# Decoder layer with 32 experts: tail order, last turn and gate product moved

## The chip, the core and the metric

The kernel runs on one core of a Trainium2 chip. The metric is device time in microseconds of one execution of the whole layer. TensorE (PE) multiplies, VectorE (DVE) and ScalarE (ACT) work on tiles elementwise, GpSimd (POOL) does elementwise work and issues the indirect DMAs, SyncE (SP) issues the loads of weights.

## What is computed

One decoder layer on 512 tokens of 1024 features, float32 (cut to the steps that matter here):

```python
proj = x @ w_in                                   # 1024 x 2048
mix = concat(pool_mixer(..), conv_mixer(..)) @ w_out
x = layer_norm(ALPHA * x + mix, ln1_g, ln1_b)
# top 4 of 32 experts per token, softmax over the chosen logits
gu = xb @ w_gate_up[e] + b_gate_up[e]             # 1024 x 2048
gate = min(gu[:, :1024], 7.0)
up = clip(gu[:, 1024:], -7.0, 7.0)
y = ((up + 1) * (gate * sigmoid(1.702 * gate))) @ w_down[e] + b_down[e]
x = layer_norm(ALPHA * x + sum of gate-weighted y, ln2_g, ln2_b)
g = sigmoid(x @ ple_gate_w + ple_gate_b)
x = layer_norm(ALPHA * x + g * (p @ ple_proj), ln3_g, ln3_b)
```

## The kernel before

**Precision and chunks.** Every float32 product is made of three float32r products: an operand is cast to a high part, the rest is its low part, and `mm3` (lines 212 to 214) issues high x low, low x high and high x high. Weights arrive in chunks of 1 MB (128 x 2048) through a ring of 14 buffers. `split` turns a chunk into two parts: ScalarE casts it (line 114) and VectorE subtracts (line 117, the "chunk subtraction"); `split(later=True)` gives the subtraction back to be called later. `ahead(j)` gives chunk j's buffers free, loads further chunks and splits as many as the lookahead allows. The order of instructions on each engine is the order of the program (a hand-made schedule), so where a call stands decides what waits behind what.

**Start.** Four token tiles of x are turned on PE (`turned`, line 309) into the high part `xh` and the low part `xl`, through two PSUM buffers of the tag `tr`; `columns` multiplies a block of w_in with them.

**Experts.** For each expert e up to 96 token rows are gathered (`gather`, line 315, GpSimd), turned by PE (`split_t`) and multiplied with 8 gate/up chunks (k = 0 to 7). `act` yields in steps: the gate is limited (`gm`, VectorE, line 337), `up` is copied (`h`, ScalarE, line 340) and clipped (GpSimd, line 341), `sg` is the sigmoid (ScalarE, line 346), the product `gm * sg` (line 347) runs on GpSimd, and VectorE finishes `h` (line 349). While that goes on, `down(e - 1)` multiplies the expert before with its 4 down chunks (j = 0 to 3, two column halves n each), and `emit` weighs the result into `yo` and adds it to `acc` in HBM by an indirect DMA (the "scatter", line 357). `h` of expert e is turned at k = 2 of expert e + 1. The last expert has no next one: it does `up` and the product on VectorE, and `last_turn` turns its `h` between `down(30)` and `down(31)`, with 3 warm matmuls ahead and 9 behind (`keep_warm`, line 208: matmuls whose result nobody reads).

**Side steps.** `tables` makes the index tables of the next experts in three steps; `embed_parts` turns the embedding input p in five steps (first `pgb`, then a tile each) in experts 19 and 20.

**Tail.** `embed(i)` is 12 matmuls, p times ple_proj for token tile i, `embedded` copies it out of PSUM. Then comes a loop with a run-time count (`further_blocks`, for experts with more than 96 rows; it runs zero times here), which every engine and all DMAs must have reached before it is left. Behind it the sums are read from `acc` into `x2`, `combine` adds the down bias, `second` is the second normalisation, `turn2` turns the tile, `gate` and `gated` multiply with ple_gate_w, `third` is the last normalisation.

Of the kernel before, what the change touches and what calls it, by code (L numbers as in the profile page):

```python
# [20 lines left out]
P = 128  # L21
# [4 lines left out]
E = 32  # L26
# [12 lines left out]

WARM_START, WARM_ROUTE, WARM_TURN, WARM_END = (6, 7, 7), (2, 2, 2), (3, 9), 10  # L40
TURN1 = 5
# [7 lines left out]
def tile_layer(ctx: ExitStack, tc: tile.TileContext, x, p, w_in, pool_mix, pool_scale, conv_w, w_out,  # L49
# [282 lines left out]

    def act(gp, up, work, mul=nc.gpsimd):

        gp, up = (q.rearrange("p a b -> p (a b)") for q in (gp, up))
        gm, h = work("gm"), work("h")
        nc.vector.tensor_scalar(gm, gp, LIMIT, None, op0=ALU.min)  # L337
        yield h
        if mul is nc.gpsimd:
            nc.scalar.copy(h, up)  # L340
            mul.tensor_scalar(h, h, LIMIT, -LIMIT, op0=ALU.min, op1=ALU.max)  # L341
        else:
            nc.vector.tensor_scalar(h, up, LIMIT, -LIMIT, op0=ALU.min, op1=ALU.max)
        yield
        sg = work("sg")
        nc.scalar.activation(sg, gm, AF.Sigmoid, scale=SW_ALPHA)  # L346
        mul.tensor_mul(gm, gm, sg)  # L347
        yield
        nc.vector.scalar_tensor_tensor(h, h, 1.0, gm, op0=ALU.add, op1=ALU.mult)  # L349
# [18 lines left out]
    with tc.tile_pool(name="mix", bufs=1, side=RIGHT) as q:  # L368
# [6 lines left out]
        with tc.tile_pool(name="xin", bufs=1, side=RIGHT) as xp:  # L375
# [17 lines left out]

            def columns(o, cs, b, ts_):

                wh, wl = (parts[cs[b]] if len(cs) == 2 else (q[:, :, b * P:(b + 1) * P] for q in parts[cs[0]]))
                for k in range(ND):
                    mm3(o[:, b, ts_], wh[:, k], wl[:, k], xh[:, k, ts_], xl[:, k, ts_], k == 0, k == ND - 1)

# [7 lines left out]
            o1 = big()  # L407
            columns(o1, c_in[0], 0, slice(0, 256))
            turned(2)
            turned(3)  # L410
            columns(o1, c_in[0], 1, slice(0, 256))
            for b in range(2):
# [443 lines left out]

    def embedded(i, o, halves=False):
        if halves:
            nc.scalar.copy(ple[i][:, :512], o[:, 0])
            nc.vector.tensor_copy(ple[i][:, 512:], o[:, 1])  # L860
        else:
            nc.scalar.copy(ple[i], o.rearrange("p a b -> p (a b)"))


    hs, hT = {}, {}

    def down(e, after={}, before={}):
        ah, al = hT.pop(e)
        o = big(CAP)
        for j in range(4):  # L870
            wh, wl = parts.pop(c_dn[e][j])
            for n in range(2):
                ns = slice(n * 512, (n + 1) * 512)
                for b in range(2):
                    k = 2 * j + b
                    mm3(o[:, n], ah[:, k], al[:, k], wh[:, b, ns], wl[:, b, ns], k == 0, k == ND - 1)
            for f in before.get(j, ()):
                f()
            if e == E - 2 and j == 2:
                done(c_dn[e][j])  # L880
            elif e < E - 1 or j < 3:
                ahead(c_dn[e][j])
            for f in after.get(j, ()):
                f()
# [4 lines left out]
    def last_turn():  # L889
        keep_warm(WARM_TURN[0], bsp[:, :P], bsp[:, :512])  # L890
        hT[E - 1] = split_t(hs.pop(E - 1), "x", mp1, 1)
        keep_warm(WARM_TURN[1], bsp[:, :P], bsp[:, :512])

# [11 lines left out]
    for e in range(E):  # L905
# [7 lines left out]
        for k in range(ND):  # L913
            wh, wl = parts.pop(c_gu[e][k])
            for o, n, c in halves:
                cs = slice(c, c + 512)
                mm3(o[:, n], ah[:, k], al[:, k], wh[:, 0, cs], wl[:, 0, cs], False, k == ND - 1)
            if k < ND - 1 or e:
                kept = ahead(c_gu[e][k], int(e == E - 1 and k == 0))
# [13 lines left out]
            if k == (0 if e == E - 1 else 1):  # L933
                steps = (tables(2, mp1) if e == 0 else tables(0, mp1) if e == 1 else
                         tables(e + 2, mp1) if e % 2 == 0 and e + 2 < E else
                         further() if e == 5 else prepare() if e == E - 1 else iter(()))
            if k in ((1, 2, 4) if e < E - 1 else (0, 1, 4, 5, 6)):
                next(steps, None)
            if (e, k) == (EMBED + 1, 0):
                embed_steps = embed_parts()  # L940
            if (e, k) in ((EMBED + 1, 0), (EMBED + 1, 1), (EMBED + 1, 4), (EMBED + 1, 5), (EMBED + 2, 0)):
                next(embed_steps, None)
        last = e == E - 1
        if e and not last:
            xT[e + 1] = split_t(xg.pop(e + 1), "x", mp1, 1)
        steps_h = act(gp, up, lambda n: mp2.tile([P, F], F32, tag=n, name=n)[:CAP], nc.vector if last else nc.gpsimd)
        hs[e] = next(steps_h)
        if not last:
            next(steps_h)
        if e == 0:  # L950
# [12 lines left out]
        if last:  # L963
            limit[0] = len(chunks)
            down(e - 1, {0: [finish, finish, finish]}, {3: [last_turn]})
        elif e:
            down(e - 1, {0: [multiply], 1: [gather_next], 2: [finish]})
        else:
            multiply()
            gather_next()  # L970
# [23 lines left out]
    later = []  # L994
    down(E - 1, {2: [lambda: later.append(split(later=True))]})
    later[0]()
    lookahead[0] = 5
    splits(1)
    embedded(0, embed(0))
    o1, o2 = embed(1), embed(2)  # L1000
    last_part = split(later=True)
    embedded(1, o1)
    embedded(2, o2, True)

# [63 lines left out]

    combine(0)
    combine(1)  # L1070
    o3 = embed(3)
    keep_warm(WARM_END, bsp[:, :P], bsp[:, :512], tr([P, 512]))
    last_part()
    second(0)
    embedded(3, o3)
    parts.pop(c_pp)
    done(c_pp)
    turn2(0)
    second(1)
    for i in range(NT):  # L1080
# [45 lines left out]
```

## Time and profile before

| What | Value |
|---|---|
| Median of 3 runs | 1420.75 us (1419.46 to 1421.67) |
| Profiled execution, its own time | 1419.95 us |
| Its span, first to last instruction | 1418.1 us |
| PE busy | 1390.6 us, 98% |
| VectorE busy | 1235.8 us, 87% |
| ScalarE busy | 949.6 us, 67% |
| GpSimd busy | 446.4 us, 31% |
| DMA | 464.43 MB, mean 327 GB/s |
| Granted PE clock, mean | 0.995 of full |

Busy time is a share of the whole span; a stage can be bound by another engine than the mean tells, so the rows further down are read stage by stage. Start times in them count from the start of the span. Several matmuls overlap in PE's pipeline, so the distance from start to start is what one costs.

### The profile page before, as it was taken

The page shows a single profiled execution, that of the slowest core. Times are in us where ns is not written, and L with a number is a line of the kernel's source. Part 1 is how long each engine was busy: PE and PEld are TensorE (multiplying, and loading weights), DVE is VectorE, ACT ScalarE, POOL GpSimd, SP SyncE. Part 2 cuts the span into 40 slices and gives each one's busy share as a digit, 9 for nine tenths or more (in the row PEclk, how much of TensorE's full clock was granted, in tenths as well). Part 3 has the DMA queues.
Part 4 walks back from the last instruction along what each step waited for, and adds up shares of the span by engine and source line. Part 5 has one row for each costly group of instructions (what it writes and reads, how often), then busy time and mean ns, then how long its engine had stood idle before and what let it go on. Part 6 is the DMA issues. An engine that isn't in the chain of part 4 may idle for free.

```text
span 1418.1 us, 17667 instructions
## 1 busy us (share of the span) xinstructions
PE 1390.6 (98%) x6616; PEld 994.3 (70%) x6616; DVE 1235.8 (87%) x1050; ACT 949.6 (67%) x741; POOL 446.4 (31%) x201
## 2 busy tenths in 40 slices
PE   9999999999999999999999999999999999999896
PEld 8788766666666666666666666666666666666675
DVE  6645589999999999999989998999999999999785
ACT  5321267777777777777777777777777777777631
POOL 1101124355455555555542231222222222221200
PEclk9999999999999999999999999999999999999998
DMA  9327889999999999999889999999999999999421
GB/s 331 122 89 238 327 330 350 362 383 380 367 376 385 366 380 376 375 371 379 308 311 346 385 389 358 373 377 370 377 377 379 364 379 371 375 377 340 122 90 45
DMA packets 98071, 464.43 MB, mean 327 GB/s; under 512 B 9424, under 2 KB 19168, under 8 KB 65216
## 3 DMA queue, kind: packets, MB, share of 16 engines
q1 hardware_dynamic: 86784, 428.12, 78.3%
q0 software_dynamic: 9536, 33.44, 9.5%
q10 hardware_dynamic: 1664, 1.72, 0.5%
q8 instruction: 54, 0.88, 0.2%
q14 instruction: 33, 0.27, 0.0%
HBM read 443.97 MB, written 19.27 MB: 327 GB/s over the span
## 4 chain that ended last, share of the span: by engine, by line
PE 88%; DVE 6%; issue 4%; DMA 1%; ACT 1%; POOL 0%; DVEq 0%; SPq 0%; ACTq 0%; POOLq 0%
PE big L212 27%; PE big L214 26%; PE big L213 26%; PE tr L309 4%; PE big L1050 3%; DVE ring11dt.float32r L117 1%; PE big L911 1%; DMA acc<-yo,idxs 1%; DVE ring0dt.float32r L117 1%; DVE ring1dt.float32r L117 1%; DVE ring13dt.float32r L117 1%; DVE ring3dt.float32r L117 1%; DVE ring12dt.float32r L117 1%; DMA xs<-in_x_dram 0%; PE tr L571 0%
## 5 line engine op out<-in xcount | busy, mean ns | idle before, releaser
L341 POOL TENSOR_SCALAR h<-h 96x1024 f32<-96x1024 f32 x31 | 39.8, 1283 | 572.4 <-ACT h L340 572.4
L357 POOL DMA_INDIRECT acc<-yo,idxs x32 | 178.9, 5589 | 90.9 <-ACT yo L356 84.0
L214 PE MATMUL big<-chunk,xh 128*96 128x512 f32 x480 | 189.1, 394 | 0.0
L213 PE MATMUL big<-chunk,xl 128*96 128x512 f32 x480 | 188.5, 393 | 0.0
L347 POOL TENSOR_TENSOR gm<-gm,sg 96x1024 f32<-96x1024 f32 x31 | 103.7, 3346 | 65.8 <-ACT sg L346 64.0
L214 PE MATMUL big<-chunk,hh 128*96 128x512 f32 x268 | 105.5, 394 | 0.0
L213 PE MATMUL big<-chunk,hl 128*96 128x512 f32 x268 | 105.5, 394 | 0.0
L214 PEld LDWEIGHTS big<-chunk,xh 128*96 128x96 f32 x480 | 77.1, 161 | 33.2
L213 PEld LDWEIGHTS big<-chunk,xl 128*96 128x96 f32 x480 | 77.4, 161 | 31.0
L315 POOL DMA_INDIRECT xg<-x1d,idxg x31 | 91.8, 2960 | 21.9 <-DVE idxg L655 13.7
L214 PEld LDWEIGHTS big<-chunk,hh 128*96 128x96 f32 x268 | 43.4, 162 | 19.2
L213 PEld LDWEIGHTS big<-chunk,hl 128*96 128x96 f32 x268 | 43.3, 162 | 17.6
L346 ACT ACTIVATE sg<-gm 96x1024 f32<-96x1024 f32 x32 | 34.0, 1061 | 17.9 <-DVE gm L337 13.8
L324 ACT CAST xh<-tr 128x384 fp32r<-128x384 f32 x64 | 27.5, 480 | 24.5 <-PE tr L309 24.5
L117 DVE TENSOR_TENSOR ring12dt.float32r<-ring12dt.float,ring6dt.float32r 128x2048 fp32r<-128x2048 f32 x14 | 35.3, 2521 | 7.8 <-ACT ring6dt.float32r L114 7.8
L356 ACT ACTIVATE yo<-big,gs 96x1024 f32<-96x1024 f32 x31 | 34.5, 1111 | 10.9 <-PE big L214 10.9
L349 DVE SCALAR_TENSOR_TENSOR h<-h,gm 96x1024 f32<-96x1024 f32 x32 | 38.7, 1211 | 2.6 <-POOL gm L347 2.6
L324 ACT CAST hh<-tr 128x384 fp32r<-128x384 f32 x62 | 26.6, 479 | 18.4 <-PE tr L309 18.4
L337 DVE TENSOR_SCALAR gm<-big 96x1024 f32<-96x1024 f32 x32 | 38.7, 1210 | 0.0
L117 DVE TENSOR_TENSOR ring9dt.float32r<-ring9dt.float,ring2dt.float32r 128x2048 fp32r<-128x2048 f32 x14 | 34.7, 2481 | 4.3 <-ACT ring2dt.float32r L114 4.3
L117 DVE TENSOR_TENSOR ring3dt.float32r<-ring3dt.float,ring10dt.float32r 128x2048 fp32r<-128x2048 f32 x14 | 34.7, 2481 | 4.0 <-ACT ring10dt.float32r L114 4.0
L117 DVE TENSOR_TENSOR ring1dt.float32r<-ring1dt.float,ring8dt.float32r 128x2048 fp32r<-128x2048 f32 x14 | 34.7, 2481 | 3.7 <-ACT ring8dt.float32r L114 3.7
(585 smaller groups left out, 4430.4 us busy)
## 6 DMA issues: line engine op xcount, KB each, us to landing
ring13dt.float<-in_w_gate_up_dram SPq DMA_DIRECT2D x18, 1024.0 KB, 7.1
ring10dt.float<-in_w_gate_up_dram SPq DMA_DIRECT2D x18, 1024.0 KB, 7.2
ring1dt.float<-in_w_gate_up_dram SPq DMA_DIRECT2D x18, 1024.0 KB, 6.9
ring2dt.float<-in_w_gate_up_dram SPq DMA_DIRECT2D x18, 1024.0 KB, 7.5
ring3dt.float<-in_w_gate_up_dram SPq DMA_DIRECT2D x18, 1024.0 KB, 8.0
ring4dt.float<-in_w_gate_up_dram SPq DMA_DIRECT2D x18, 1024.0 KB, 7.7
ring9dt.float<-in_w_gate_up_dram SPq DMA_DIRECT2D x17, 1024.0 KB, 7.3
ring5dt.float<-in_w_gate_up_dram SPq DMA_DIRECT2D x17, 1024.0 KB, 7.2
```

The source lines that it names most:

```text
L117: second()
L212: nc.tensor.matmul(o, ah, bl, start=start, stop=False)
L213: nc.tensor.matmul(o, al, bh, start=False, stop=False)
L214: nc.tensor.matmul(o, ah, bh, start=False, stop=stop)
L309: nc.tensor.transpose(t[:, k, :], src[:, (4 * h + k) * P:(4 * h + k + 1) * P], ident[:n, :n])
L315: nc.gpsimd.indirect_dma_start(out=xg, out_offset=None, in_=x1d, in_offset=bass.IndirectOffsetOnAxis(ap=idxg[:, e:e + 1], axis=0))
L324: nc.scalar.copy(hi[:, 4 * h:4 * h + 4], t)
L337: nc.vector.tensor_scalar(gm, gp, LIMIT, None, op0=ALU.min)
L341: mul.tensor_scalar(h, h, LIMIT, -LIMIT, op0=ALU.min, op1=ALU.max)
L347: mul.tensor_mul(gm, gm, sg)
L357: nc.gpsimd.indirect_dma_start(out=acc, out_offset=bass.IndirectOffsetOnAxis(ap=idx, axis=0), in_=y, in_offset=None, compute_op=ALU.add)
L1050: nc.tensor.matmul(o, q[a + k // 4][:, k % 4], ws[k // 2][b][:, k % 2, c0:c1], start=False, stop=b == 1 and k == ND - 1)
```

## The change

Five things are edited. `act` has one form for all experts: ScalarE copies `up`, GpSimd clips it, and the product of gate and sigmoid is VectorE's, a step after the sigmoid. `last_turn` is called within the last down chunk of expert 30, between its two column halves, without warm matmuls. In the tail two embedding tiles stand ahead of the run-time loop and two behind; of the three last chunk splits, the subtractions stand behind the last scatter, one ahead of the loop and two behind it. At the start, token tiles 2 and 3 are turned within `columns`. The steps of `embed_parts` and the third table step of expert 0 stand at other k.

```diff
-WARM_START, WARM_ROUTE, WARM_TURN, WARM_END = (6, 7, 7), (2, 2, 2), (3, 9), 10
+WARM_START, WARM_ROUTE, WARM_END = (6, 7, 7), (2, 2, 2), (8, 3)
...
-        if mul is nc.gpsimd:
-            nc.scalar.copy(h, up)
-            mul.tensor_scalar(h, h, LIMIT, -LIMIT, op0=ALU.min, op1=ALU.max)
-        else:
-            nc.vector.tensor_scalar(h, up, LIMIT, -LIMIT, op0=ALU.min, op1=ALU.max)
+        nc.scalar.copy(h, up)
+        nc.gpsimd.tensor_scalar(h, h, LIMIT, -LIMIT, op0=ALU.min, op1=ALU.max)
         yield
         sg = work("sg")
         nc.scalar.activation(sg, gm, AF.Sigmoid, scale=SW_ALPHA)
-        mul.tensor_mul(gm, gm, sg)
+        yield
+        nc.vector.tensor_mul(gm, gm, sg)
...
-            columns(o1, c_in[0], 0, slice(0, 256))
-            turned(2)
-            turned(3)
-            columns(o1, c_in[0], 1, slice(0, 256))
+            columns(o1, c_in[0], 0, slice(0, 256), {4: 2})
+            columns(o1, c_in[0], 1, slice(0, 256), {2: 3})
...
     def last_turn():
-        keep_warm(WARM_TURN[0], bsp[:, :P], bsp[:, :512])
         hT[E - 1] = split_t(hs.pop(E - 1), "x", mp1, 1)
-        keep_warm(WARM_TURN[1], bsp[:, :P], bsp[:, :512])
...
-            if k in ((1, 2, 4) if e < E - 1 else (0, 1, 4, 5, 6)):
+            if k in ((0, 1, 4, 5, 6) if e == E - 1 else (1, 2, 4 if e else 6)):
                 next(steps, None)
...
-            if (e, k) in ((EMBED + 1, 0), (EMBED + 1, 1), (EMBED + 1, 4), (EMBED + 1, 5), (EMBED + 2, 0)):
+            if (e, k) in ((EMBED + 1, 0), (EMBED + 1, 4), (EMBED + 1, 5), (EMBED + 3, 4), (EMBED + 3, 5)):
                 next(embed_steps, None)
...
-            down(e - 1, {0: [finish, finish, finish]}, {3: [last_turn]})
+            down(e - 1, {0: [finish] * 3}, {(3, 0): [last_turn]})
         elif e:
-            down(e - 1, {0: [multiply], 1: [gather_next], 2: [finish]})
+            down(e - 1, {0: [multiply], 1: [multiply, gather_next], 2: [finish]})
...
     down(E - 1, {2: [lambda: later.append(split(later=True))]})
-    later[0]()
-    lookahead[0] = 5
-    splits(1)
-    embedded(0, embed(0))
-    o1, o2 = embed(1), embed(2)
-    last_part = split(later=True)
-    embedded(1, o1)
-    embedded(2, o2, True)
+
+    embedded(0, embed(0), nc.vector.tensor_copy)
+    lookahead[0] = 5
+    later.append(split(later=True))
+    o = embed(1)
+    later.append(split(later=True))
+    embedded(1, o)
+    later[0]()
+    keep_warm(WARM_END[0], bsp[:, :P], bsp[:, :512], tr([P, 512]))
...
     combine(0)
+    o2 = embed(2)
+    embedded(2, o2)
     combine(1)
     o3 = embed(3)
-    keep_warm(WARM_END, bsp[:, :P], bsp[:, :512], tr([P, 512]))
-    last_part()
+    keep_warm(WARM_END[1], bsp[:, :P], bsp[:, :512], tr([P, 512]))
+    later[1]()
     second(0)
     embedded(3, o3)
...
     turn2(0)
+    later[2]()
     second(1)
```

The rows that follow are instructions in program order of one engine: line, operation, output<-inputs, shape.

VectorE in a late expert (27), from the limit of the gate (`gm`) to the finished `h`; the `ring` rows are chunk subtractions. Before:

```order
L337 TENSOR_SCALAR gm<-big 96x1024
L117 TENSOR_TENSOR ring10dt.float32r<-ring10dt.float_83,ring12dt.float32r 128x2048
L117 TENSOR_TENSOR ring1dt.float32r<-ring1dt.float_65,ring8dt.float32r 128x2048
L117 TENSOR_TENSOR ring2dt.float32r<-ring2dt.float_67,ring13dt.float32r 128x2048
L349 SCALAR_TENSOR_TENSOR h<-h,gm 96x1024
```

And after:

```order
L337 TENSOR_SCALAR gm<-big 96x1024
L117 TENSOR_TENSOR ring10dt.float32r<-ring10dt.float_83,ring12dt.float32r 128x2048
L117 TENSOR_TENSOR ring1dt.float32r<-ring1dt.float_65,ring8dt.float32r 128x2048
L345 TENSOR_TENSOR gm<-gm,sg 96x1024
L117 TENSOR_TENSOR ring2dt.float32r<-ring2dt.float_67,ring13dt.float32r 128x2048
L347 SCALAR_TENSOR_TENSOR h<-h,gm 96x1024
```

The product now stands on VectorE between two chunk subtractions, and the second of these behind it.

PE from the last down chunk of expert 30 to the first of expert 31: `hh` and `xh` are the turned h of expert 30 and 31, `tr` the transposes. Before:

```order
L212 MATMUL big<-ring0dt.float32r,hh 96x512
L213 MATMUL big<-ring3dt.float32r,hl 96x512
L214 MATMUL big<-ring3dt.float32r,hh 96x512
L208 MATMUL big<-bsp 128x512 x3
L309 MATMUL tr<-ident,h 128x96 x8
L208 MATMUL big<-bsp 128x512 x9
L212 MATMUL big<-ring6dt.float32r,xh 96x512
```

And after:

```order
L309 MATMUL tr<-ident,h 128x96 x8
L212 MATMUL big<-ring0dt.float32r,hh 96x512
L213 MATMUL big<-ring3dt.float32r,hl 96x512
L214 MATMUL big<-ring3dt.float32r,hh 96x512
L212 MATMUL big<-ring0dt.float32r,hh 96x512
L213 MATMUL big<-ring3dt.float32r,hl 96x512
L214 MATMUL big<-ring3dt.float32r,hh 96x512
L212 MATMUL big<-ring6dt.float32r,xh 96x512
```

The eight transposes moved ahead of six products of expert 30, and the twelve warm matmuls are gone.

VectorE from the last `yo` (which the last scatter sends) to the sums of token tile 1; the rows of the run-time loop are left out. Before:

```order
L354 TENSOR_SCALAR yo_1441<-big,gs 96x512
L996 TENSOR_TENSOR ring10dt.float32r<-ring10dt.float_83,ring9dt.float32r 128x2048
L117 TENSOR_TENSOR ring1dt.float32r<-ring1dt.float_65,ring11dt.float32r 128x2048
L860 COPY after<-big 128x512
...
L1073 TENSOR_TENSOR ring2dt.float32r<-ring2dt.float_67,ring3dt.float32r 128x2048
L276 SCALAR_TENSOR_TENSOR x_9739,mv<-x_9739,big 128x512 x2
...
L1040 TENSOR_TENSOR turned_9799<-tr,turned_9797 128x512
L1040 TENSOR_TENSOR turned_9800<-tr,turned_9798 128x512
L276 SCALAR_TENSOR_TENSOR x_9740,mv<-x_9740,big 128x512 x2
```

And after:

```order
L352 TENSOR_SCALAR yo_1441<-big,gs 96x512
L856 COPY after<-big 128x1024
L999 TENSOR_TENSOR ring10dt.float32r<-ring10dt.float_83,ring9dt.float32r 128x2048
...
L1072 TENSOR_TENSOR ring1dt.float32r<-ring1dt.float_65,ring11dt.float32r 128x2048
L276 SCALAR_TENSOR_TENSOR x_9719,mv<-x_9719,big 128x512 x2
...
L1037 TENSOR_TENSOR turned_9786<-tr,turned_9784 128x512
L1037 TENSOR_TENSOR turned_9787<-tr,turned_9785 128x512
L1078 TENSOR_TENSOR ring2dt.float32r<-ring2dt.float_67,ring3dt.float32r 128x2048
L276 SCALAR_TENSOR_TENSOR x_9720,mv<-x_9720,big 128x512 x2
```

Of the three chunk subtractions one stayed ahead of the loop, behind the copy of embedding tile 0, and two stand behind the loop, the last of them between the turned tile 0 and the sums of tile 1.

## Rows read from the trace of the kernel before

**Rows 1.** Windows: us; busy (count) of PE, PEld, DVE, ACT, POOL; PE clock; DMA.

```profile
380.70:737.12 356.42, 356.42 (x1681) 248.37 (x1680) 335.23 (x226) 268.86 (x190) 185.03 (x40) 1.00 0.99 369
887.13:1245.72 358.59, 357.25 (x1683) 248.17 (x1682) 333.87 (x227) 271.32 (x191) 91.11 (x43) 1.00 1.00 374
860.10:864.00 3.90, 3.90 (x14) 2.71 (x15) 3.06 (x3) 0.48 (x1) 0.00 (x0) 0.62 1.03 432
```

**Rows 2.** PE's waits, longest first: total us, times, longest.

```profile
PE big L1023 <- issue: 4.3, 1, 4.3
PE tr L309 <- DVE p L845: 2.5, 1, 2.5
PE tr L309 <- DVE xl L391: 1.0, 1, 1.0
PE tr L309 <- DVE tabsb L623: 0.7, 1, 0.7
```

**Rows 3.** The chain that ended last: first and last of its 15 late subtractions.

```profile
773.03 3.67 DVE ring11dt.float32r L117
1279.58 3.64 DVE ring11dt.float32r L117
```

**Rows 4.** Timeline of VectorE, GpSimd and TensorE in one late expert.

```profile
1170.51 3.25 POOL L347 TENSOR_TENSOR gm<-gm,sg 96x1024 f32<-96x1024 f32 x1 [2.39 <-ACT sg L346]
1174.04 2.74 POOL L315 DMA_INDIRECT xg<-x1d,idxg  x1 [0.27 <-POOL gm L347]
1172.26 3.66 DVE L117 TENSOR_TENSOR ring1dt.float32r<-ring1dt.float,ring8dt.float32r 128x2048 fp32r<-128x2048 f32 x1 [0.78 <-ACT ring8dt.float32r L114]
1175.85 2.28 DVE L117 TENSOR_TENSOR ring2dt.float32r<-ring2dt.float,ring13dt.float32r 128x2048 fp32r<-128x2048 f32 x1
1178.82 0.40 PE L212 MATMUL big<-ring2dt.float32r,xh 128*96 128x512 f32 x1
```

**Rows 5.** Timeline around the last h and the last down products.

```profile
1317.74 0.85 PE L208 MATMUL big<-bsp 128*128 128x512 f32 x3
1319.03 2.32 PE L208 MATMUL big<-bsp 128*128 128x512 f32 x9
1318.96 0.86 ACT L324 CAST xh<-tr 128x384 fp32r<-128x384 f32 x2 [4.26 <-PE tr L309]
1321.67 2.29 DVE L117 TENSOR_TENSOR ring11dt.float32r<-ring11dt.float,ring9dt.float32r 128x2048 fp32r<-128x2048 f32 x1 [1.07 <-ACT ring9dt.float32r L114]
1324.01 0.47 PE L212 MATMUL big<-ring11dt.float32r,xh 128*96 128x512 f32 x1
```

**Rows 6.** Timeline around the last scatter, and the earlier scatter of expert 29.

```profile
1334.03 2.28 DVE L996 TENSOR_TENSOR ring10dt.float32r<-ring10dt.float,ring9dt.float32r 128x2048 fp32r<-128x2048 f32 x1
1336.22 2.28 DVE L117 TENSOR_TENSOR ring1dt.float32r<-ring1dt.float,ring11dt.float32r 128x2048 fp32r<-128x2048 f32 x1
1285.29 1.48 POOL L357 DMA_INDIRECT acc<-yo,idxs  x1 [4.23 <-ACT yo L356]
1334.38 5.42 POOL L357 DMA_INDIRECT acc<-yo,idxs  x1 [6.91 <-DVE yo L354]
1341.41 0.69 DVE L860 COPY after<-big 128x512 f32<-128x512 f32 x1 [2.91 <-ACT after L859]
```

**Rows 7.** The chain that ended last, at the last scatter.

```profile
1334.38 9.23 DMA acc<-yo,idxs
```

**Rows 8.** Timeline behind the run-time loop.

```profile
1345.06 1.53 PE L1023 MATMUL big<-bd,gt 96*128 96x512 f32 x4 [4.30 <-issue]
1352.71 1.25 PE L309 MATMUL tr<-ident,x 128*128 128x128 f32 x8
1355.22 0.68 DVE L276 SCALAR_TENSOR_TENSOR x<-x,big 128x512 f32<-128x512 f32 x1
1358.95 1.41 DVE L300 SCALAR_TENSOR_TENSOR x<-work,mv,after 128x512 f32<-128x512 f32 x2 [0.67 <-POOL mv L293]
1359.91 1.23 PE L309 MATMUL tr<-ident,x 128*128 128x128 f32 x8
```

More of the change, by code (lines that the diff above doesn't have):

```diff
@@ L331, in split_t, with act @@
         return both
-    def act(gp, up, work, mul=nc.gpsimd):
+    def act(gp, up, work):
         gp, up = (q.rearrange("p a b -> p (a b)") for q in (gp, up))
@@ L392, in turned, with columns @@
                 transposed(xs[i], P, put)
-            def columns(o, cs, b, ts_):
+            def columns(o, cs, b, ts_, between={}):
                 wh, wl = (parts[cs[b]] if len(cs) == 2 else (q[:, :, b * P:(b + 1) * P] for q in parts[cs[0]]))
                 for k in range(ND):
+                    if k in between:
+                        turned(between[k])
                     mm3(o[:, b, ts_], wh[:, k], wl[:, k], xh[:, k, ts_], xl[:, k, ts_], k == 0, k == ND - 1)
@@ L855, in embed, with embedded, down @@
         return o
[L857 to L862, printed above, removed]
+    def embedded(i, o, copy=nc.scalar.copy):
+        copy(ple[i], o.rearrange("p a b -> p (a b)"))
     hs, hT = {}, {}
-    def down(e, after={}, before={}):
+    def down(e, after={}, between={}):
         ah, al = hT.pop(e)
@@ L876, in down @@
                     mm3(o[:, n], ah[:, k], al[:, k], wh[:, b, ns], wl[:, b, ns], k == 0, k == ND - 1)
-            for f in before.get(j, ()):
-                f()
+                for f in between.get((j, n), ()):
+                    f()
             if e == E - 2 and j == 2:
@@ L917, in tile_layer @@
                 mm3(o[:, n], ah[:, k], al[:, k], wh[:, 0, cs], wl[:, 0, cs], False, k == ND - 1)
-            if k < ND - 1 or e:
+            if (e, k) == (E - 1, ND - 1):
+                done(c_gu[e][k])
+            elif k < ND - 1 or e:
                 kept = ahead(c_gu[e][k], int(e == E - 1 and k == 0))
@@ L945, in tile_layer @@
             xT[e + 1] = split_t(xg.pop(e + 1), "x", mp1, 1)
-        steps_h = act(gp, up, lambda n: mp2.tile([P, F], F32, tag=n, name=n)[:CAP], nc.vector if last else nc.gpsimd)
+        steps_h = act(gp, up, lambda n: mp2.tile([P, F], F32, tag=n, name=n)[:CAP])
         hs[e] = next(steps_h)
-        if not last:
-            next(steps_h)
+        next(steps_h)
+        if last:
+            splits()
         if e == 0:
@@ L964, in tile_layer @@
             limit[0] = len(chunks)
-            down(e - 1, {0: [finish, finish, finish]}, {3: [last_turn]})
+            down(e - 1, {0: [finish] * 3}, {(3, 0): [last_turn]})
         elif e:
-            down(e - 1, {0: [multiply], 1: [gather_next], 2: [finish]})
+            down(e - 1, {0: [multiply], 1: [multiply, gather_next], 2: [finish]})
         else:
+            multiply()
             multiply()
```

## The prediction

> **What bounds the kernel now.** I read the windows first: two stretches of ten experts, one early and one late [rows 1]. In the early one PE is busy for all of its 356.42 us at the full clock; in the late one it is busy for 357.25 of 358.59 us. So the experts are bound by TensorE, and a change helps only where PE waits or does filler work. Next I read PE's waits [rows 2]: 4.3 us behind the run-time loop, 2.5 us in the expert that turns the embedding input, 1.0 us at the start, 0.7 us in expert 0. Third, the chain that ended last [rows 3]: it stays on PE except at 15 points, one per expert from 773 to 1280 us, where a chunk subtraction of VectorE takes about 3.65 us instead of the usual 2.28. Last I read the timeline at the end, where the last scatter must land before the sums can be read back, and that is where filler matmuls stand.
>
> **Gate product on VectorE.** The timeline of one late expert shows why that subtraction is long [rows 4]. GpSimd's product runs from 1170.51 to 1173.76; the subtraction has started at 1172.26 and ends at 1175.92, 2.16 after the product's end, which is nearly its whole own length. It was held, not slowed. The change takes the product off GpSimd (3.25) and puts one on VectorE (an estimate of 1.2: half the width of a subtraction of 2.28). VectorE gives 3.66 - 2.28 = 1.38 back and gets 1.2, so its load hardly changes. What matters is the order: the held subtraction now ends at about 1174.54, before PE asks for it, and the product comes behind it. The next one, of ring2, then starts at about 1175.7 instead of 1175.85, and PE needs it at 1178.82. The gain is the difference of the two stretches: (358.59 - 356.42)/10 = 0.22 per expert, 15 times: **-3.3**. Bounds: 0, if another wait steps in, and -3.3, since PE is busy throughout the early stretch and no more is to be had. The gather now waits for VectorE's product, but its rows are wanted only at the end of the next expert.
>
> **Embedding input turned later.** In expert 19 the second piece (a cast, a subtraction, two transposes) no longer follows right behind the first. PE waited 2.5 us there for a transpose buffer [rows 2], and for 3.90 us behind it PE ran at a granted clock of 0.62 [rows 1], which loses 3.9 x 0.38 = 1.5. The pieces now stand at k = 4 and 5 of experts 19 and 21; in the kernel before, two stood at k = 4 and 5 of 19, and no wait of PE is listed for them. **-4.0**, bounds -2.5 and -4.3.
>
> **Start and expert 0.** The transposes of the last two x tiles are spread between column products, with 18 products between the two, so the buffers are free again: the 1.0 wait goes. The table step of expert 0 moves from k = 4 to 6, behind the transposes that waited 0.7 for its buffer. **-1.7**, bounds 0 and -2.7 (two shorter waits near by).
>
> **The last h.** Twelve warm matmuls go. From 1317.74 to 1324.01 lie 12 of them, 8 transposes (some 0.6) and 12 products [rows 5], so each is about 0.23 and the twelve are 2.8. But the second down chunk gives only part of it back: its subtraction starts at 1321.67 and ends at 1323.96, and PE takes it at 1324.01, at once. That subtraction hangs on a cast of ScalarE that stood idle 4.26 us for the transposes. They move up by six products and three warm matmuls, 2.1. Against that h gets a longer way: ScalarE copies it, GpSimd clips it, and two chunk subtractions stand before the product; I reckon h ready about 0.2 behind the point where PE wants it. **-1.9**, bounds 0 and -2.8.
>
> **The last scatter.** It takes GpSimd 5.42, while two chunk subtractions run back to back on VectorE until 1338.50; it ends 1.30 later. An earlier scatter, beside the step that finishes h, took 1.48 [rows 6]. So I read that the subtractions hold it. They now stand behind: one after the copy of embedding tile 0 out of PSUM, which itself waits for 12 matmuls (2.8) behind the last down product, and two after the run-time loop. That would end the scatter 3.9 earlier, and its landing, 9.23 behind its start [rows 7], with it. The Trainium skill's page "SBUF — State Buffer", section "Who interferes with whom", speaks against this: there a tensor-tensor operation takes only the shared read side, while descriptors of GpSimd's DMAs need the write side (the page marks that as inferred), and none was seen to stall. By that page this term is 0. The row stands nearer to this case, so I take most of 3.9.
>
> The loop's exit also wants every engine. The last to arrive before is VectorE's copy, until 1342.10 [rows 6]; after, it is PE. Its filler ended at 1340.76 before (1345.06 less 4.30 idle) [rows 8]; 32 matmuls in place of 36, begun 1.9 earlier, end at about 1337.9. If arrival decides, both steps together give 4.2; if the landing decides, 1.9 + 3.9 = 5.8. I take **-5.0** for last h and scatter together. Behind the loop PE now does 4 + 24 + 3 matmuls instead of 4 + 12 + 10, 31 x 0.23 = 7.1, with a wait of about 0.8 between for a copy out of the buffer that the last tile takes; from 1345.06 to 1352.71 it had 7.65, so this term is near 0, and up to +1.5 if the clock falls there as it did in expert 19.
>
> **The subtraction behind the first turned tile.** Before, VectorE starts the sums of tile 1 at 1355.22, without a gap, and ends them at 1360.36; PE asked for them at 1359.91 [rows 8]. One chunk subtraction (2.28, pitch 2.2) is now in front of them. Nothing covers it: PE waits about 2.1 longer. **+2.1**, bounds 0 and +2.3.
>
> **Sum.** -3.3 - 4.0 - 1.7 - 5.0 + 2.1 = -11.9. The profiled execution took 1419.95 (span 1418.1 and 1.85 around it), so 1408.05; it lies 0.8 under the median of 1420.75, so I forecast 1408.8.
>
> **Rivals.** (a) The subtractions do not hold the scatter, as that page would have it. For it: another cause of 5.42 isn't excluded by one row. Against it: the end 1.30 behind the last subtraction. Then 3.1 of the 5.0 is lost (last h alone remains): 1411.9. (b) The loop's gain is not had, because VectorE, busy 333.87 of 358.59, lets another subtraction come late: 1412.1. (c) The sums of tile 1 come in time, since PE is later there than I think: 1406.7. (d) **Slower**: GpSimd's gather now begins when the product on VectorE ends, beside the ring2 subtraction, and takes the memory side first, as the product did. That subtraction would then be held by up to 2.74, end at about 1180.6 and make PE wait 1.8 in each expert without slack, 15 times: +27, less the 8.6 of the other terms, 1439. It decides from 0.6 us of wait per expert on. Against it: the gather before (1174.04 to 1176.78) runs beside that same subtraction, which takes its plain 2.28 [rows 4]. (e) The change doesn't do what it says, but in expert 19: the late subtractions stay late (0 for -3.3), the start's wait moves on to the next buffer (0 for -1.7), h comes late by all that the warm matmuls gave and the scatter isn't freed (0 for -5.0). Then -4.0 + 2.1 is left, 1418.8, no change.
>
> **Chances.** Forecast with its own spread 0.61, (a) 0.15, (b) 0.09, (c) 0.08, (d) 0.04, (e) 0.03. The range takes in the forecast, (a), (b) and (c): 1404.5 ((c) with the loop's exit by the landing, -0.8, and the lower bounds of start and expert 19, -1.3) to 1413.5 ((a) with a fall of the clock behind the loop, 1.5). About 0.2% (2.8 us) is what a measurement of this kernel can tell from no change: faster 0.93, same 0.03, slower 0.04.
>
> **What would show it.** In the late stretch, chunk subtractions of 2.28 and none of 3.6, and 356.4 us for ten experts. No wait for the embedding input near 857 and no low clock behind it. The last scatter at about 1.5 on GpSimd and the loop left some 5 earlier. Then a wait of about 2 at the second turned tile, as the one step that costs. The forecast is wrong if the last scatter still takes over 4, if a late subtraction stays over 3, or if PE shows new waits per expert.

## The result and the profile after

| What | Before | After |
|---|---|---|
| Median, us | 1420.49 (1419.46 to 1421.67) | 1411.35 (1411.05 to 1414.0) |
| Ratio to before | | 0.994 (0.9928 to 0.9952) |
| Profiled execution, own time | 1419.95 | 1411.42 |
| Its span | 1418.1 | 1409.6 |
| PE busy | 1390.6 | 1388.1 |
| VectorE busy | 1235.8 | 1228.7 |

The change gives 9.1 us. The forecast was 1408.8, 2.6 us lower, in a range from 1404.5 to 1413.5. By the time alone the result lies nearer to the rivals (a), 1411.9, and (b), 1412.1, than to the forecast, so the profile has to tell them apart. PE's waits after the change (wait, total, times, longest):

```profile
PE big L1020 <- issue: 2.3, 1, 2.3
PE tr L309 <- issue: 2.0, 1, 2.0
...
PE big L903 <- ACT h L339: 0.7, 1, 0.7
PE big L212 <- ACT after L856: 0.6, 1, 0.6
...
PE tr L640 <- DVE xl L325: 0.6, 1, 0.6
```

Of the waits of before [rows 2], those for the embedding input, for the low part of x and for the table are gone (one of 0.6 has come at the table's own matmuls, line 640), and the one behind the loop fell from 4.3 to 2.3. A new one of 2.0 stands at the transposes, "issue", since the profile saw no release for it: the second turned tile.

The start of an expert's bias products on PE is a good mark, since it is the same four matmuls in both kernels. Experts 2, 17, 19, 20 and 31, before:

```profile
240.17 0.70 PE L911 MATMUL big<-bsp,sel 64*96 64x512 f32 x4
...
775.91 0.70 PE L911 MATMUL big<-bsp,sel 64*96 64x512 f32 x4
...
847.61 0.70 PE L911 MATMUL big<-bsp,sel 64*96 64x512 f32 x4
...
888.21 0.70 PE L911 MATMUL big<-bsp,sel 64*96 64x512 f32 x4
...
1282.46 0.70 PE L911 MATMUL big<-bsp,sel 64*96 64x512 f32 x4
```

And after:

```profile
238.02 0.70 PE L903 MATMUL big<-bsp,sel 64*96 64x512 f32 x4
...
774.65 0.70 PE L903 MATMUL big<-bsp,sel 64*96 64x512 f32 x4
...
846.00 0.70 PE L903 MATMUL big<-bsp,sel 64*96 64x512 f32 x4
...
881.92 0.70 PE L903 MATMUL big<-bsp,sel 64*96 64x512 f32 x4
...
1274.35 0.70 PE L903 MATMUL big<-bsp,sel 64*96 64x512 f32 x4
```

The differences of the marks, and of marks in the tail, split the 8.5 us of the two spans:

| Stretch | Before | After | Difference | Predicted |
|---|---|---|---|---|
| to expert 2 | 240.17 | 238.02 | -2.15 | -1.7 |
| experts 2 to 16 | 535.74 | 536.63 | +0.89 | 0 |
| experts 17 and 18, 20 to 30 | 465.95 | 463.78 | -2.17 | with 19: |
| expert 19 | 40.60 | 35.92 | -4.68 | -7.3 |
| expert 31's start to the last scatter | 51.92 | 50.04 | -1.88 | -1.9 |
| last scatter to PE behind the loop | 10.68 | 7.77 | -2.91 | -3.1 |
| PE behind the loop to turned tile 0 | 7.65 | 8.14 | +0.49 | 0 |
| turned tile 0 to turned tile 1 | 7.20 | 9.37 | +2.17 | +2.1 |
| turned tile 1 to the end | 58.19 | 59.93 | +1.74 | 0 |

The tail of the kernel after, as a timeline (start, length, engine, line and instruction, in brackets the idle time before it):

```profile
1324.39 1.41 POOL L355 DMA_INDIRECT acc<-yo,idxs  x1 [6.90 <-DVE yo L352]
...
1327.90 1.97 PE L208 MATMUL tr<-bsp 128*128 128x512 f32 x8
...
1332.16 0.73 PE L1020 MATMUL big<-bd,gt 96*128 96x512 f32 x2 [2.29 <-issue]
...
1340.30 1.33 PE L309 MATMUL tr<-ident,x 128*128 128x128 f32 x8
...
1342.89 2.28 DVE L1078 TENSOR_TENSOR ring2dt.float32r<-ring2dt.float,ring3dt.float32r 128x2048 fp32r<-128x2048 f32 x1
...
1345.09 0.68 DVE L276 SCALAR_TENSOR_TENSOR x<-x,big 128x512 f32<-128x512 f32 x1
...
1348.82 1.41 DVE L300 SCALAR_TENSOR_TENSOR x<-work,mv,after 128x512 f32<-128x512 f32 x2 [0.67 <-POOL mv L293]
...
1349.67 1.33 PE L309 MATMUL tr<-ident,x 128*128 128x128 f32 x8 [1.95 <-issue]
```

The scatter takes 1.41 instead of 5.42 [rows 6], and PE is back 7.77 behind its start. Then the subtraction of line 1078 runs until 1345.17, the sums of tile 1 start at 1345.09 and finish from 1348.82 on, and PE, done with its 24 products, has stood idle for 1.95. The end of the chain shows what follows (start, length, what):

```profile
1342.06 5.68 PE big L1047 x24
1347.73 1.94 issue
1351.89 7.22 PE big L1047 x24
```

The first 24 products take 5.68, the 24 behind the wait 7.22. Windows show the clock (columns as in [rows 1], the granted clock third from the end):

```profile
887.13:1245.72 358.59, 358.59 (x1693) 250.19 (x1692) 333.64 (x239) 272.41 (x193) 159.49 (x34) 1.00 1.01 379
1332.70:1336.00 3.30, 3.30 (x15) 2.44 (x13) 1.41 (x3) 0.30 (x1) 0.00 (x0) 1.00 0.74 218
1342.06:1347.73 5.67, 5.66 (x24) 4.35 (x24) 5.57 (x10) 1.25 (x3) 0.00 (x0) 1.00 0.02 7
1351.89:1355.30 3.41, 3.41 (x9) 2.70 (x9) 3.30 (x10) 0.00 (x0) 0.00 (x0) 0.52 0.00 0
```

The first row is the late stretch: PE is now busy for all of it. The next two are the products right behind the loop and those behind the first turned tile, at the full clock of 2.4 GHz; in the last, behind the idle 1.95, the granted clock is 0.52, nearly all of it at the lower level of 1.2 GHz. The 24 products lose 1.5 us by it, which the sum didn't have.

In a late expert, VectorE and GpSimd read:

```profile
1164.67 2.29 DVE L117 TENSOR_TENSOR ring1dt.float32r<-ring1dt.float,ring8dt.float32r 128x2048 fp32r<-128x2048 f32 x1 [0.72 <-ACT ring8dt.float32r L114]
...
1166.88 1.21 DVE L345 TENSOR_TENSOR gm<-gm,sg 96x1024 f32<-96x1024 f32 x1
...
1168.01 2.28 DVE L117 TENSOR_TENSOR ring2dt.float32r<-ring2dt.float,ring13dt.float32r 128x2048 fp32r<-128x2048 f32 x1
...
1168.94 12.61 POOL L315 DMA_INDIRECT xg<-x1d,idxg  x1 [8.36 <-DVE gm L345]
```

The subtraction of 3.66 [rows 4] takes 2.29, and none of the experts' subtractions is over 3 us any more. In the kernel before there were 15 such late ones, and 15 more in the early experts, most of 3.96, which a reading of the critical chain doesn't show: there PE had slack. The gather starts behind VectorE's product, as foreseen, but it is the gather that is long now, 12.61 instead of 2.74, beside a run of VectorE operations that take their usual time. It is needed so late that PE doesn't wait for it.

### The profile page after: what moved, and what is told of

Its sections match the earlier page's. It is cut to its first block, busy times and chain, and to the rows that moved or that the text cites. A ratio compares the mean times of both kernels' runs of the same rounds, so it can differ in the third digit from the quotient of the medians.

```text
span 1409.6 us, 17694 instructions
## 1 busy us (share of the span) xinstructions
PE 1388.1 (98%) x6605; PEld 994.1 (71%) x6605; DVE 1228.7 (87%) x1080; ACT 949.8 (67%) x741; POOL 446.3 (32%) x171
## 5 line engine op out<-in xcount | busy, mean ns | idle before, releaser
L315 POOL DMA_INDIRECT xg<-x1d,idxg x31 | 203.7, 6570 | 253.9 <-DVE gm L345 184.8
L355 POOL DMA_INDIRECT acc<-yo,idxs x32 | 169.7, 5304 | 39.7 <-ACT yo L354 23.9
L293 POOL TENSOR_TENSOR mv<-mv,mhalf 128x1 f32<-128x1 f32 x12 | 7.8, 651 | 99.1 <-DVE mv L292 86.0
L345 DVE TENSOR_TENSOR gm<-gm,sg 96x1024 f32<-96x1024 f32 x32 | 38.9, 1215 | 0.1
L339 ACT COPY h<-big 96x1024 f32<-96x1024 f32 x32 | 32.6, 1020 | 5.6 <-PE big L214 5.6
L117 DVE TENSOR_TENSOR ring12dt.float32r<-ring12dt.float,ring6dt.float32r 128x2048 fp32r<-128x2048 f32 x14 | 32.0, 2286 | 4.5 <-ACT ring6dt.float32r L114 4.5
```

Of the source, the lines that this page charges most:

```text
L117: second()
L315: nc.gpsimd.indirect_dma_start(out=xg, out_offset=None, in_=x1d, in_offset=bass.IndirectOffsetOnAxis(ap=idxg[:, e:e + 1], axis=0))
L345: nc.vector.tensor_mul(gm, gm, sg)
L355: nc.gpsimd.indirect_dma_start(out=acc, out_offset=bass.IndirectOffsetOnAxis(ap=idx, axis=0), in_=y, in_offset=None, compute_op=ALU.add)
```

## Experiments

The baseline in the first two is the changed kernel (1411.35); times are medians.

**1. Both subtractions ahead of the first sums**

```diff
     later[1]()
+    later[2]()
     second(0)
 ...
     turn2(0)
-    later[2]()
     second(1)
```

> The changed kernel with the third chunk subtraction moved: it follows the second one, ahead of the first sums, instead of standing between the turned tile 0 and the sums of tile 1. Theory (the wait at the second turned tile comes from that subtraction, and the fall of PE's clock behind it from the wait): in the changed kernel PE stood idle 1.95 us and then ran 24 products in 7.22 instead of 5.66, so both go and about 3.5 us come back, 1407.9, with no wait of over 0.5 at that place. VectorE has 0.78 and 1.40 us of idle time ahead of the two sums of tile 0, so these are not late. Rival A (the sums of tile 0 become late by the moved 2.28): PE waits ahead of the first turned tile instead, 1410 to 1411.5. Rival B (PE's second turned tile is late for another reason than VectorE's order): no change, 1411.4.

Measured: 1407.45 (1407.34 to 1408.9), ratio to before 0.9912 (0.9899 to 0.9926), as the theory said. From the chain:

```profile
1342.85 5.65 PE big L1047 x24
1348.50 0.57 PE tr L309 x4
```

The second turned tile follows its 24 products at once. One thing was not foreseen: in this execution the clock fell behind the run-time loop,

```profile
1332.30:1336.50 4.20, 4.20 (x13) 3.27 (x13) 4.16 (x7) 0.00 (x0) 0.00 (x0) 0.63 0.90 295
```

though PE's pause there was 2.37, against 2.29 in the changed kernel, whose clock stayed full. That fall lengthens the stretch from PE's return to the first turned tile from 8.14 to 9.60. From the first turned tile to the end this execution takes 65.40 instead of 69.31: the step's 3.9 come back. The 3.9 between the medians is the same figure, but this execution, 1408.63, isn't the median one.

**2. Filler in the wait**

```diff
+        if i == 0:
+            keep_warm(9, bsp[:, :P], bsp[:, :512], tr([P, 512]))
         if more_tiles:
             turn2(i + 1)
```

> The changed kernel with nine filler matmuls (9 x 0.23 = 2.1 us) ahead of the second turned tile, where PE waits 1.95 us. The wait of PE's results stays, only PE does not stand idle in it. Theory (1.56 us of the tail are the clock, not the wait): the 24 products behind it take 5.7 instead of 7.22, 1.4 to 1.6 us faster, 1409.9. Rival (those products are slow because VectorE, ScalarE or a PSUM buffer is late): no change or 0.1 to 0.2 slower, 1411.5.

Measured: 1411.01 (1410.21 to 1412.02), inconclusive as a time. The chain shows that the mechanism holds:

```profile
1348.96 2.05 PE tr L208 x9
...
1353.31 5.64 PE big L1047 x24
```

With PE kept busy the 24 products behind take 5.64 instead of 7.22: in the changed kernel they were slow by the clock. But in this execution the clock fell behind the loop instead (0.62 in 1332.70 to 1336.50, after a pause of 2.28), which moved the wait 1.4 later. A profile told the two apart, the median did not.

**3. Gate product alone**, on the kernel before:

```diff
-        mul.tensor_mul(gm, gm, sg)
+        if mul is nc.gpsimd:
+            yield
+        nc.vector.tensor_mul(gm, gm, sg)
...
-            down(e - 1, {0: [multiply], 1: [gather_next], 2: [finish]})
+            down(e - 1, {0: [multiply], 1: [multiply, gather_next], 2: [finish]})
         else:
+            multiply()
```

> The kernel before with one thing changed: the product of gate and sigmoid is VectorE's, one down chunk after the sigmoid, in all experts but the last. Theory (the held subtraction cost PE 0.22 us in each of 15 late experts): 3.3 us faster, 1417.2, with late subtractions of 2.28, ten late experts in 356.4 us. Rival A: VectorE's product costs PE some time in every expert, early ones too, as the changed kernel's profile hints (ten early experts 0.7 us longer there than before): 1.5 to 2.4 us faster, 1418.1 to 1419, and ten early experts in 357.1. Rival B (none of the gain belongs to it): 1420.5.

Measured: 1415.66 (1415.28 to 1416.94), ratio 0.9969 (0.9957 to 0.9981): 4.6 us, more than the theory's 3.3, which its interval (2.7 to 6.1) takes in. The marks of experts 2, 17 and 31:

```profile
238.91 0.47 PE L913 MATMUL big<-bsp,sel 64*96 64x512 f32 x2
...
774.64 0.70 PE L913 MATMUL big<-bsp,sel 64*96 64x512 f32 x4
...
1278.39 0.70 PE L913 MATMUL big<-bsp,sel 64*96 64x512 f32 x4
```

From expert 2 to 17 it takes 535.73, as before: rival A falls. From 17 to 31 it takes 503.75 instead of 506.55, so 0.20 for each of 14 experts, near the predicted 0.22 for each of 15. The early subtractions were held as well, and longer, but there the hold cost PE nothing. Of the rest, 1.0 comes in expert 1: expert 2's mark is 1.26 earlier, and 0.25 of that stood at expert 0's own mark already. Two waits of PE in expert 1, 0.29 for a chunk subtraction (213.43) and 0.34 for the table's one-hot tile (219.70), are gone; the gate product's term did not count them.

**4. Two subtractions back behind the scatter**, on the changed kernel:

```diff
+    later[0]()
+    lookahead[0] = 5
+    splits(1)
     embedded(0, embed(0), nc.vector.tensor_copy)
-    lookahead[0] = 5
     later.append(split(later=True))
     o = embed(1)
-    later.append(split(later=True))
     embedded(1, o)
-    later[0]()
 ...
-    later[1]()
 ...
-    later[2]()
+    later[1]()
```

> The changed kernel with two chunk subtractions put back right behind the last scatter, back to back, ahead of the copy of embedding tile 0; the third stays behind the turned tile 0. Theory (subtractions that run back to back hold the scatter): the scatter takes GpSimd about 5.4 us instead of 1.41, lands some 4 later, PE stands idle for about 6 in the loop instead of 2.3 and loses some clock behind it: 3.5 to 6 us slower, 1415 to 1417.5. Rival (the scatter was long for another reason, the subtractions do not hold it): the scatter stays below 2 us, and the time changes by at most 1 us either way.

Measured: 1415.85 (1414.77 to 1417.79), 4.5 slower than the changed kernel. Timeline of VectorE, GpSimd and PE:

```profile
1324.16 2.28 DVE L993 TENSOR_TENSOR ring10dt.float32r<-ring10dt.float,ring9dt.float32r 128x2048 fp32r<-128x2048 f32 x1
...
1326.36 2.28 DVE L117 TENSOR_TENSOR ring1dt.float32r<-ring1dt.float,ring11dt.float32r 128x2048 fp32r<-128x2048 f32 x1
...
1324.52 5.41 POOL L355 DMA_INDIRECT acc<-yo,idxs  x1 [6.90 <-DVE yo L352]
...
1335.30 1.22 PE L1020 MATMUL big<-bd,gt 96*128 96x512 f32 x2 [5.30 <-issue]
```

The scatter is back at 5.41, ends 1.29 behind the second subtraction as in [rows 6], and PE's pause is 5.30. The subtractions hold it: rival (a) of the prediction falls. PE is back 1.44 behind the scatter's landing.

**5. Last h turned as before**, on the changed kernel: `{(3, 1): [last_turn]}` for `{(3, 0): ...}`, with 3 warm matmuls ahead and 9 behind. The last expert's other edits stay: its `up` is copied by ScalarE and clipped by GpSimd, and a split behind its last chunk stands later (`splits()` behind `next(steps_h)`), which the list of five edits ahead of the prediction leaves out.

> The changed kernel with the last h turned where it was before: behind both column halves of the last down chunk of expert 30, with 3 warm matmuls ahead of the transposes and 9 behind. Theory (the turn within the down products gives the terms of the prediction, 1.9, and the profile of the changed kernel gives 2.0 between expert 31's first product and its last): 1.9 to 2.3 us slower, 1413.3 to 1413.7. Rival (h is ready so late that the earlier turn only moves the wait): below 0.8 us slower, 1412.

Measured: 1413.14 (1410.95 to 1416.1), 1.8 slower, with a wide spread that overlaps the baseline, so the time alone doesn't show it. The profile gives 1.65: the last scatter starts 51.69 behind expert 31's mark instead of 50.04.

**6. Table step of expert 0 back at k = 4**, on the changed kernel: `(1, 2, 4)` for `(1, 2, 4 if e else 6)`.

> The changed kernel with the third table step of expert 0 back at k = 4. In the profiles the stretch of expert 0 is 0.18 shorter in the changed kernel than in the one with the gate product alone, and each expert from 2 to 16 is 0.05 to 0.07 longer, with the same instructions. Theory (the step takes the wait of 0.7 away and has nothing to do with the 0.07): 0.2 to 0.7 us slower, 1411.6 to 1412.1, ten early experts as long as in the changed kernel, 357.1. Rival (the place of the step decides how buffers fall in all experts behind it, and with it the 0.07): 0.3 to 0.8 us faster, 1410.6, ten early experts in 356.4.

Measured: 1411.89 (1409.94 to 1412.77), no difference by the time. The marks of experts 6 and 16, in the changed kernel,

```profile
381.68 0.71 PE L903 MATMUL big<-bsp,sel 64*96 64x512 f32 x4
...
738.81 0.70 PE L903 MATMUL big<-bsp,sel 64*96 64x512 f32 x4
```

and with the step at k = 4:

```profile
381.38 0.70 PE L903 MATMUL big<-bsp,sel 64*96 64x512 f32 x4
...
737.81 0.70 PE L903 MATMUL big<-bsp,sel 64*96 64x512 f32 x4
```

Ten experts take 357.13 there and 356.43 here, the value of the kernel before. The rival holds: 0.9 us over experts 2 to 16 comes with the place of a step in expert 0, whose own gain is 0.2. In this execution the clock fell behind both pauses of the tail, which hid it in the time.

**7. Start as before**, on the changed kernel: the two calls of `turned` between the column blocks.

> The changed kernel with token tiles 2 and 3 of x turned between the two column blocks, as before. Theory (the wait of 1.0 us for the low part of x at the start comes back, and nothing else): 0.8 to 1.2 us slower, 1412.2 to 1412.6, ten early experts in 357.1 as in the changed kernel. Rival (the order at the start decides the longer early experts): the wait comes back, but ten early experts take 356.4, and the time stays within 0.3 of 1411.4.

Measured: 1412.71 (1410.57 to 1415.35), 1.4 slower, with a wide spread that overlaps the baseline; in the profile PE's wait for the low part of x is back with 1.0, and the long early experts stay. Expert 0's mark stands at 175.69 to 176.34 in the five profiles with the old start, at 174.31 to 174.97 in the nine with the new one. The theory holds by the profile. This profile also bears on the clock: PE waits 2.12 at the second turned tile, and the products behind the wait run at the full clock,

```profile
1354.30:1358.00 3.70, 3.70 (x16) 2.73 (x15) 3.65 (x9) 0.47 (x1) 0.00 (x0) 1.00 0.02 4
```

so such a wait doesn't bring a fall in every execution.

**8. The two subtractions in another form**, on the kernel before: `scalar_tensor_tensor(lo, t, 1.0, hi, mult, subtract)` for `tensor_sub(lo, t, hi)`.

> The kernel before with the two chunk subtractions behind the last scatter written as scalar-tensor-tensor operations (x * 1.0 - high part) in place of tensor-tensor ones, same inputs and output. Theory A (any operation of VectorE that streams two float32 inputs from SBUF without a pause holds the scatter): the scatter stays near 5.4 us and the time at 1420.3. Rival B (only the tensor-tensor form holds it, as an earlier scatter that ran beside a scalar-tensor-tensor step took 1.48): the scatter takes about 1.5, lands some 3.9 earlier, and the time falls by 1.5 to 4 us.

Measured: 1421.22 (1417.88 to 1422.02), ratio 1.0005 (0.9996 to 1.0014). Timeline:

```profile
1334.05 2.28 DVE L999 SCALAR_TENSOR_TENSOR ring10dt.float32r<-ring10dt.float,ring9dt.float32r 128x2048 fp32r<-128x2048 f32 x1
...
1336.25 2.28 DVE L120 SCALAR_TENSOR_TENSOR ring1dt.float32r<-ring1dt.float,ring11dt.float32r 128x2048 fp32r<-128x2048 f32 x1
...
1334.41 5.43 POOL L360 DMA_INDIRECT acc<-yo,idxs  x1 [6.91 <-DVE yo L357]
```

The scatter takes 5.43. The form of these two operations doesn't matter: rival B falls. Theory A, that any such neighbour holds the scatter, goes too far, as the trace of the kernel before shows. Its 15 scatters from 778 to 1286 us take 1.47 to 1.52 though VectorE has no gap beside them; each starts 0.05 to 0.09 ahead of the step of VectorE that finishes `h` (line 349). Its 13 scatters from 277 to 707 us start 0.10 to 0.44 behind the start of that same step and take 8.73 to 11.40, for instance

```profile
384.70 1.21 DVE L349 SCALAR_TENSOR_TENSOR h<-h,gm 96x1024 f32<-96x1024 f32 x1
...
385.14 11.39 POOL L357 DMA_INDIRECT acc<-yo,idxs  x1 [1.70 <-ACT yo L356]
```

So the moment at which the scatter starts goes with the hold; no experiment moved that moment alone.

**9. Table tiles taken first.** On the kernel of experiment 1; the instructions stay in place, only the tiles `tabsb` and `tabwk` are taken from the pool earlier:

```diff
             onehot(oh[-1], rk1[:, :, e:e + 1])
+            if e > e0:
+                sb, wk = decode_tiles(2, pool)
             yield
 ...
-        decode(tab, 2, idxg[:, es], idxs[:, es], gs[:, es], pool)
+        decode(tab, 2, idxg[:, es], idxs[:, es], gs[:, es], sb, wk)
```

> The kernel with both subtractions ahead of the first sums (1407.45) and one thing more: the two small tiles that the table step decodes into are taken from their pool at k = 2 of expert 0, so they lie ahead of the turned x in SBUF as in the kernel before; every instruction keeps its place, the table step stays at k = 6. Theory (the 0.05 to 0.07 us that each of the experts 2 to 16 costs more comes from where tiles lie in SBUF, which follows from the order in which they are first taken): it is gone, ten early experts in 356.4, 1.0 us faster in all, 1406.4. Rival (it comes from the order of the instructions around the table step): ten early experts in 357.1 as before the edit, 1407.4.

Marks of experts 6 and 16:

```profile
381.47 0.70 PE L907 MATMUL big<-bsp,sel 64*96 64x512 f32 x4
...
737.90 0.70 PE L907 MATMUL big<-bsp,sel 64*96 64x512 f32 x4
```

Ten experts take 356.43: the 0.07 is gone, so the order in which the tiles are taken causes it, and not the place of an instruction. The time, 1407.89 (1406.72 to 1408.21), doesn't show the 0.9 against 1407.45; the first mark came 0.6 later in this profile than in experiment 1, and the tail's clock differs from execution to execution.

**10 and 11. Fewer warm matmuls**, on the kernel of experiment 9: `WARM_END = (8, 0)`, then `(3, 0)`.

> As the run before, without the three warm matmuls ahead of the first turned tile behind the loop. In the profile of the kernel with both subtractions first, PE's clock fell behind the loop and PE was the last there (turn at 1341.39, the first half of its input finished at about 1340.5). Theory: up to 0.7 us less where the clock falls, nothing where it does not, 0.3 us faster on the median. Rival (the pause ahead of the turn lets the clock fall behind it): 0.5 to 1.5 slower.

> As the run before, with three warm matmuls instead of eight ahead of the run-time loop, so that PE arrives there 1.2 us earlier. Theory (the last to arrive at the loop is PE's filler, at 1329.87 in the changed kernel): the loop is left up to 0.8 us earlier, until the landing of the scatter decides (1329.6 to 1329.9), and the clock then falls behind it in every execution, which costs up to 1.4: between 0.5 faster and 0.8 slower. Rival (the scatter's landing decides already): the loop is left at the same time, PE stands idle 3.5 there, 0.5 to 1 slower.

Measured: 1406.04 (1405.82 to 1407.34), ratio 0.9902 (0.9887 to 0.9917), and 1406.47 (1406.01 to 1406.97). The first is 1.9 faster than experiment 9 by the medians, more than the theory's 0.3; in its profile the clock stayed full behind the loop (1.00 in 1330.70 to 1334.00), which can be part of it. The second bears on the loop's exit:

```profile
1326.10 0.84 PE L208 MATMUL tr<-bsp 128*128 128x512 f32 x3
...
1329.22 0.85 PE L1024 MATMUL big<-bd,gt 96*128 96x512 f32 x2 [2.28 <-issue]
```

The last filler matmul ends at 1326.94 and PE is back at 1329.22, 2.28 later; in experiment 10 1328.40 and 1330.63, 2.23, and in the changed kernel 1329.87 and 1332.16, 2.29. VectorE ends at 1327.00 and is back at 1329.19, 2.19 later, and in experiment 10 at 1327.33 and 1329.52, 2.19 again, though PE comes to the loop only at 1328.40 there. So where the scatter is early, PE and VectorE are each back some 2.2 to 2.4 behind their own last instruction, and the loop is not left by all engines at once, as the text ahead of the prediction has it. Where the scatter is late (the kernel before, experiments 3, 4, 8 and 12), PE is back 1.44 to 1.46 behind its landing. In experiment 11 both bounds meet: the scatter lands at 1327.76, 1.46 ahead of PE's return, so this profile alone doesn't tell which of them holds PE. The theory's gain at the exit is there, 1.4 for PE, but brings little: the first sums stand behind VectorE's two subtractions and start at 1333.60 instead of 1333.93, and PE's clock fell behind its pause (0.55 from 1329.30 to 1333.00).

**12. Embedding steps alone**, on the kernel before: the tuple of (e, k) as in the change.

> The kernel before with one thing changed: the five steps that turn the embedding input stand at k = 0, 4, 5 of expert 19 and k = 4, 5 of expert 21. Theory (the prediction's term of 4.0; the changed kernel's profile gives 4.5 back at expert 19 and takes 0.4 again at expert 21): 4.0 faster, 1416.3, no wait for the embedding input near 857 and no low clock behind it. Rival (what is given back at expert 19 only moves a later wait): less than 2 us faster, above 1418.3.

Measured: 1416.59 (1415.64 to 1417.29), ratio 0.9974 (0.9965 to 0.9984), 3.9 faster, as the theory said. PE no longer waits for the embedding input, and its granted clock from 860 to 864 is 1.00.

## Why the prediction was right, and where a size was off

That the time came so near is partly luck: a gain of 1.0 in expert 1 and a loss of 0.9 in experts 2 to 16 were both missed and cancel, and the clock in the tail can move the time by more than 1 us either way. So each term is judged by itself.

**Gate product, -3.3.** Right in mechanism, and near in size: 2.8 in the late experts. The subtraction was held, as read from [rows 4]; experiment 3 isolates it, and rival (b) falls. The term counted 15 stretches, and 14 lie between the marks of 17 and 31. Its 1.0 in expert 1 was missed. Rival (d), a gather that takes the memory side from the ring2 subtraction, fell: the gather is what grew, and that subtraction took 2.28.

**Embedding input, -4.0.** Right: 3.9 alone. The two pieces moved to expert 21 cost 0.4, and expert 19 gave 4.6.

**Start and expert 0, -1.7.** The start gives its 1.0 (the wait, experiment 7; expert 0's mark is 1.01 earlier). The table step gives 0.2, since its matmuls now wait 0.6 for their PSUM buffer, and loses 1.0 in experts 1 to 16; its share of the term had the wrong sign.

**Last h and last scatter, -5.0.** Right: 1.88, of which experiment 5 gives 1.65 to the place of the turn, and 2.91. That the loop waits for the last engine to arrive was wrong (experiments 10 and 11): before, the scatter's landing held PE, and now PE's own 2.3. So neither of the two exits reckoned, 4.2 and 5.8, is what happened; that the 5.0 chosen between them meets the 4.8 measured is in part luck. The scatter term rested on one row against a rule, and experiments 4 and 8 settle it for this place; the scatter of 1.48 that the prediction set beside it started just ahead of VectorE's step, not within it. The Trainium skill's page "SBUF — State Buffer", section "Who interferes with whom", leaves a tensor-tensor operation out of what starves descriptor generation; here two such operations cost the scatter 4.0 us, and a gather grew from 2.74 to 12.61. By that sentence of the page the scatter's part of this term would have been 0.

**The subtraction behind the first turned tile, +2.1, bounds 0 and +2.3.** This is the step that was mis-sized; rival (c), that it costs nothing, falls. The wait came as reckoned (1.95 idle, +2.17 by the marks); but the sum priced the pause only, and the clock fell behind it: 24 products in 7.22 instead of 5.66, and 1.74 to the end. With the fall the step costs 3.9, and experiment 1, which removes it, gives 3.9 back. In experiment 7 the same wait came without the fall, so 2.1 to 3.9 is its price by execution, and a bound of +2.3 was too low. The price stood in the rows: the sum counted 1.5 for exactly this in expert 19, and named it behind the loop as a bound, but not here.

**Behind the loop, near 0.** It is +0.49. PE waits 0.64 for the copy of embedding tile 2 out of PSUM, which the prediction had counted with 0.8; its own 7.1 + 0.8 against 7.65 already makes +0.25. The 7.65 of before held a fall of the clock (0.58 in 1345.06 to 1349.06), and the clock stayed full here in the changed kernel's profile. Of the nine profiles with an early scatter seven show a fall at this place, so a full clock there was luck; experiment 1 shows +1.46 more with it.

The terms off are then +1.7 (clock), +0.9 (experts 2 to 16), +0.5 (behind the loop), and some smaller ones of both signs; they make the 3.4 between the sum of -11.9 and the 8.5 of the spans.

## What to carry to other kernels

Where a forecast adds a pause of some 2 us to a full PE, give it two prices, the pause alone and the pause with slower products behind it, and if the pause can't be avoided, try to fill it. Where an indirect DMA is on the path, look at what VectorE does as it starts: one that started within a run of back-to-back subtractions was held until the run ended, and moving the run behind it freed it. And where a stretch changes in length with the same instructions in it, look at what changed in the order in which tiles are taken.

## What the runs showed of the hardware

- The clock behind a pause of PE of about 2 us is not settled. Behind the loop it stayed full after 2.29 in the changed kernel and 2.23 in experiment 10, and fell after 2.28 (0.62) and 2.37 (0.63) in experiments 2 and 1 and in five more profiles. At the second turned tile it fell after 1.95 to 0.52 in the changed kernel, and stayed full after 2.12 in experiment 7. In experiment 1 the executions with a mean granted clock of 0.996 took 1408.63 and 1408.90, those with 0.998 took 1407.34 to 1407.45.
- An indirect scatter that takes 1.41 us with VectorE idle at its start takes 5.4 when it starts within two back-to-back subtractions, in either instruction form, and ends 1.3 behind the second. Early scatters of the kernel before, started within longer runs, took up to 11.40; late ones, started 0.05 to 0.09 ahead of VectorE's next operation, took 1.5. What lets those through is open.
- A subtraction of 2.28 that starts while GpSimd multiplies two tiles took 3.66 and ended 2.16 behind the product's end; with the product on VectorE none is held.
- With the same instructions, ten experts take 356.43 or 357.13 us, by the order in which small tiles were taken from a pool (experiments 6 and 9); from expert 16 on there is no difference. Where in SBUF the tiles came to lie was not read out, and why it slows the products is open.
